# A trunk of three token mixers: gate columns taken beside the RWKV scan, pooling and retention taken as pairs of block products behind it

## The chip, the cores and the metric

One core of one Trainium2 chip runs the whole program. The metric is the device time of one execution in microseconds (us). The kernel before took 2242.8 us as the median of three runs (2242.8 to 2242.94). Engines go by the profile's names: PE is TensorE's matmuls, PEld its weight loads, DVE is VectorE, ACT is ScalarE, POOL is GpSimd, and SP issues all DMAs.

## The reference

Two layers and a final RMSNorm on a sequence of 1024 positions with 1024 channels, float32. A layer is:

```
h = rms_norm(x, norm_g) * (1 + scale) + shift
proj = h @ w_in
o_pool = causal_pool_mixer(pool_u, pool_w, pool_scale) * silu(pool_g)
o_ret  = retention(q, k, v, positions, ret_norm_g) * silu(ret_g)
o_rwkv = rwkv7_time_mix(rw, ...) * silu(rw_g)
y = einsum('btnw,nwd->btnd', stack(o_pool, o_ret, o_rwkv), w_branch)
merged = sum(sigmoid(gate_logits) * y, over branches)
x = x + gate * (merged @ w_out)
```

`proj` has 13 columns of tiles for RWKV (lora, and k, r, v of four pairs of heads), 8 for pooling, 16 for retention (q, k, v and a gate for each of four heads), 4 for the gate of RWKV's output, and 24 for the gate logits. RWKV's state is a recurrence over time. Here it runs in 16 chunks of 64 positions for each pair of heads.

## The kernel before, in words

All large products are float32 kept as a high and a low part (`split`: ACT casts the high part, POOL or DVE subtracts it), so one product of two tiles takes three matmuls of 128x128 by 128x512. A column of w_in is an *item*: `("rq", 2)`, `("gate", 1, 5)` and so on. An item alone (`in_tile2`) is 2 halves of the sequence x 8 tiles x 3 = 48 wide matmuls. Two items together (`forms`) go as a 2x2 block product by 7 instead of 8 block products (`prod`, 12 wide matmuls each), so a pair takes 84 in place of 96. The sums that this needs of the activations (`form`, tiles `T`, `thi`, `tlo`) and of the weights (`wforms`, tiles `wsum`) are made on DVE. The output of a pair ends in PSUM tiles `acc` (three banks in a ring), which `evac` reads out.

A layer goes through these stages. (1) *Scan*: `plan_layer` gives the items lora and k, r, v of the next pair of heads, and, as filler between the steps of the scan, single items. Before, those are pooling's two and retention's four items of each group and head, with the work that follows on them (`pool_task`, `ret_task`). (2) *Pairs*: 14 pairs, before from the 24 gate items and the 4 items of RWKV's output gate. (3) *Branches*: the three branch outputs by w_branch, then the output product.

`rwkv_task` runs one pair of heads: `prepare` (decays, normed keys, from the lora product `lw`), `place` and `scores` (tiles AR, BK, BKt, Z, G), `invert` and `blocks` (the triangular inverse), then the loop of 16 steps. A step is a chain over three engines: PE `two<-S,AR`, DVE `xst`, PE `ch<-xst,G`, ACT `Z`, PE `ch<-Z,BKt`, DVE `S`. The next pair's task begins when this one is done. The big tiles come from four buffers of tag `r8` (AR, BK, BKt, Z, MT: five tiles through four buffers) and one of tag `G`. The smaller ones come from `t_ri` (14), `t_mi` (8) and `t_mo` (4).

The text's order is not the program's order. Each call is recorded as an `Op` with a lane, and `Log.plan` then lists all of them again for five engines, by readiness and a key (place in the text plus a bias of its lane; `rwkv` goes first), with costs of its own. Every recorded instruction is issued in `emit`, so they all carry one line (L550) in the profile. The cost list of `Log.times` has no entry for a load of ACT's function tables, which is put in after the order is set. SP's DMAs are ordered by the same list.

Of the kernel before, what the change touches and what calls it, by code (L numbers as in the profile page):

```python
# [17 lines left out]
P = 128  # L18
D = 1024
T = 1024  # L20
L = 2
# [77 lines left out]
EARLY = (0, 0, 0, 0, 0)  # L99
# [21 lines left out]
RATE = 0.0027  # L121
HOT = ("rwkv", "hot", "lead")
# [3 lines left out]
class Op:  # L126
    __slots__ = (
        "eng", "calls", "port", "outs", "ins_", "lane", "key", "n", "late", "allocs", "after", "took",
        "left", "users", "ready", "start", "end", "occ", "dur", "inst", "no_dep", "own_dep", "idx", "big", "since", "flex", "held", "behind",
# [78 lines left out]
class Log:  # L208


    def __init__(self, nc, tc):
# [7 lines left out]
        self.quiet = None  # L219
        self.real = {"DVE": nc.vector, "POOL": nc.gpsimd}  # L220
# [6 lines left out]
    def call(self, eng, name, real, a, k):  # L227
# [11 lines left out]
        else:  # L239
# [3 lines left out]
            o.no_dep = o.own_dep = o.behind = None  # L243
            o.held = False
# [98 lines left out]
    def plan(self):  # L343
# [32 lines left out]
        for o in todo:  # L376
            o.occ, o.dur = self.times(o)
            o.big = o.eng == "PE" and len(o.calls) == 1 and o.n == "matmul" and o.calls[0][2]["rhs"].dtype == F32R
            o.key = o.idx + BIAS.get(o.lane, 0)
# [184 lines left out]
def trunk_kernel(ctx, tc, xT, cvec, pos, vecs, consts, w_ada, w_all, pool_w, lora_w, out):  # L564
# [407 lines left out]
    keep_w = {}  # L972

# [4 lines left out]
    def plan_layer(l):  # L978
        yield from [("lora",)] + RW(0)
        pools = deque(PL(i) for i in range(4))  # L980
        gates = deque(GT(0, *range(8)) + GT(1, *range(8)) + GT(2, *range(8)))
        done = 0
        while done < 4 or prog.get((l, 3), 0) < 10 or pools:
            if done < 4 and prog.get((l, done), -1) >= 0:
                done += 1
                if done < 4:
                    yield from RW(done)
                if l == 0 and done == 1:
                    yield from pools.popleft()
                yield from RT(done - 1)  # L990
            elif pools and 4 - len(pools) <= done and len(lanes["mix"]) < 2:
                yield from pools.popleft()
            elif 24 - len(gates) < EARLY[done]:
                yield gates.popleft()
            else:
                yield ("idle",)
        yield ("merge",)
        while lanes["rwkv"]:
            yield gates.popleft() if len(gates) > 24 else ("idle",)
        for _ in range(len(gates) % 2):  # L1000
            yield gates.popleft()
        rest = list(gates) + [("wg", i) for i in range(4)]
# [296 lines left out]

    def rwkv_task(l, hp, kT, rT, vp, lt):  # L1300
# [5 lines left out]
        nc.gpsimd.memset(Gf[:, 32 * P : 32 * P + 1], 0.0)  # L1306
        qa = lambda b: slice(64 + 32 * b, 96 + 32 * b)
        BKt = r8("BKt").rearrange("p (c n) -> p c n", n=P)
        Z = r8("Z").rearrange("p (c n) -> p c n", n=P)
# [3 lines left out]
        jt = lambda t, rows, c: t[rows, c, :, :].rearrange("p j t -> p (j t)")  # L1313
        bvs, rks = [], []
        kept_ = [None, None]

        def prepare(h):
            yield wait(*lt[h])
            pss = [mx("lw"), mx("lw")]
            lora_mm(pss, lw, lt[h])  # L1320
# [38 lines left out]
            kept_[h] = Ep, Em, kkn, ka  # L1359

        def place(h):
            cr = slice(8 * h, 8 * h + 8)
            Ep, Em, kkn, ka = kept_[h]
# [5 lines left out]
            for par in range(2):  # L1369
# [14 lines left out]
            nc.vector.scalar_tensor_tensor(  # L1384
                BK[:, cr, 0, :], c3(kkn), -0.5, c3(Em), op0=ALU.mult, op1=ALU.mult
            )
            yield pace()
            nc.vector.tensor_tensor(BK[:, cr, 1, :], c3(ka), c3(Em), op=ALU.mult)
            whole[h] = max(at(AR), at(BK))
            rk = ka  # L1390
            yield pace()
            nc.vector.scalar_tensor_tensor(rk, rT[h], vv(l, "r_k", hp), ka, op0=ALU.mult, op1=ALU.mult)
            yield wait(rk)
            rkh = t_ri("rkh", F32R)
            nc.scalar.copy(rkh, rk)
            rkl = t_ri("rkl", F32R)
            nc.gpsimd.tensor_tensor(rkl, rk, rkh.bitcast(F32), op=ALU.subtract)
            rks.append((rkh, rkl))
# [12 lines left out]
        def scores(h):  # L1411
            yield max(until(whole[h] + 1000), wait(Z, spare=600))
            for q in range(2):
# [3 lines left out]
                with nc.together():  # L1417
                    for c in range(n):
                        trans(ps[:, c * P : (c + 1) * P], jt(BK, slice(0, P), c0 + c), timed=True)
# [3 lines left out]
            with nc.together():  # L1423
                for j in range(8):
                    for hd in range(2):
# [3 lines left out]
                            gps[j // 4 * 2 + hd][:, o : o + P], jt(BK, rows, 8 * h + j), jt(AR, rows, 8 * h + j), timed=True  # L1429
# [9 lines left out]
        yield from prepare(0)  # L1439
        yield from prepare(1)  # L1440
        yield from place(0)
        yield from side(scores(0), place(1))
        nc.gpsimd.memset(Z[0:64, :, :], 0.0)
        yield from scores(1)
        prog[(l, hp)] = 0
        MT = r8("MT")
        M, T1, Lo = two[0:64, :], MT[0:64, 0:1024], MT[0:64, 1024:2048]
        AV = MT[64:128, :]
        T13 = T1[0:32, :].rearrange("p (u s) -> p u s", s=32)
        start = [0.0]  # L1450

        def back(b):
            q = slice(32 * b, 32 * b + 32)
            nc.vector.transpose(
                out=G[q, :, qa(b)].rearrange("p u t -> p t u"), in_=M[q, :].rearrange("p (t s) -> p t s", s=32)
            )

        def invert():
            for b in range(2):
                q = slice(32 * b, 32 * b + 32)  # L1460
                yield pace()
                nc.vector.transpose(
                    out=Lo[q, :].rearrange("p (t s) -> p t s", s=32),
                    in_=G[q, :, qa(b)].rearrange("p u t -> p t u"),
# [71 lines left out]
        for S in SS:  # L1536
            nc.gpsimd.memset(S, 0.0)
# [3 lines left out]
        def outputs(c, cy, behind=None):  # L1541
            if c % 8 == 0:
                ys[c // 8] = t_ri("y")
# [1057 lines left out]
```

## Time and profile before

| | |
|---|---|
| median of the runs | 2242.8 us |
| the profiled execution | 2243.38 us |
| its span, first to last instruction | 2241.6 us |
| PE busy | 2199.1 us, 98% |
| DVE busy | 1661.7 us, 74% |
| ACT busy | 969.0 us, 43% |
| POOL busy | 620.5 us, 28% |
| DMA, mean over the span | 111 GB/s |

The stages of layer 0 lie at about 112 to 652 us (scan), 652 to 929 us (pairs) and 929 to 1120 us (branches, output); those of layer 1 at 1176 to 1740, 1740 to 2012 and 2012 to 2184 us. The granted clock is 1.00, TensorE's upper level of 2.4 GHz, from 112 us to 2184 us. Busy times of PE are modelled, so 98% says that PE has matmuls in hand, and the stretches in which it has none are its idle time.

### The profile page before, as it was taken

How to read it: one execution, taken by the hardware profiler on the slowest of the kernel's cores; microseconds unless marked ns; L12 is line 12 of the kernel's file. 1: busy time of each engine (PE TensorE's matmuls, PEld its weight loads, DVE VectorE, ACT ScalarE, POOL GpSimd, SP SyncE). 2: the span in 40 equal slices, each digit the busy share in tenths (PEclk: the TensorE clock that was granted, in tenths of full speed). 3: DMA queues.
4: the chain of work that ended last, by engine and by line, in shares of the span. 5: the costliest groups of instructions: out<-in, count | busy, mean ns of one | idle time of the engine just before them, and what ended most of it. 6: DMA issues, size and time to landing. Idle time of an engine off the chain costs nothing. (4 is left out here: it accounts for less than half of the span.)

```text
span 2241.6 us, 34653 instructions
## 1 busy us (share of the span) xinstructions
PE 2199.1 (98%) x12788; PEld 1831.4 (82%) x12788; DVE 1661.7 (74%) x2896; ACT 969.0 (43%) x1863; POOL 620.5 (28%) x551
## 2 busy tenths in 40 slices
PE   6999999999999999999999999999999999999998
PEld 5787888888888888888878888888888888888887
DVE  6897888789587764759888788787877644465895
ACT  5636344452344444414464444435334444451254
POOL 2232324233364321420032142233435300041100
PEclk9999999999999999999999999999999999999999
DMA  9212111112146653754450111111213333356343
GB/s 320 70 46 79 39 41 39 50 60 94 50 134 212 211 194 118 239 174 148 139 180 26 49 34 49 43 43 49 85 49 108 123 112 113 113 186 229 116 141 113
DMA packets 139193, 247.77 MB, mean 111 GB/s; under 512 B 15760, under 2 KB 21136, under 8 KB 139024
## 3 DMA queue, kind: packets, MB, share of 16 engines
q1 hardware_dynamic: 139024, 245.56, 34.1%
q8 instruction: 101, 1.65, 0.3%
q14 instruction: 68, 0.56, 0.1%
HBM read 185.99 MB, written 59.51 MB: 110 GB/s over the span
## 5 line engine op out<-in xcount | busy, mean ns | idle before, releaser
L550 PE MATMUL acc<-hhi,wh 128*128 128x512 f32 x1408 | 565.3, 402 | 1.5 <-DVE rot L550 0.8
L550 PE MATMUL acc<-hhi,wl 128*128 128x512 f32 x1408 | 566.2, 402 | 0.0
L550 PE MATMUL acc<-hlo,wh 128*128 128x512 f32 x1408 | 563.5, 400 | 0.0
L550 POOL TENSOR_TENSOR wl<-wr,wh 128x512 fp32r<-128x512 f32 x139 | 185.7, 1336 | 464.6 <-ACT wh L550 332.1
L550 PEld LDWEIGHTS acc<-hhi,wh 128*128 128x128 f32 x1408 | 265.6, 189 | 47.7 <-DVE rot L550 2.0
L550 PEld LDWEIGHTS acc<-hlo,wh 128*128 128x128 f32 x1408 | 265.4, 189 | 45.3
L550 PEld LDWEIGHTS acc<-hhi,wl 128*128 128x128 f32 x1408 | 265.3, 189 | 44.7
L550 ACT CAST wh<-wr 128x512 fp32r<-128x512 f32 x210 | 129.6, 617 | 247.1 <-PE acc L550 175.1
L550 PE MATMUL acc<-T,wh 128*128 128x512 f32 x672 | 208.3, 390 | 0.0
L550 POOL TENSOR_TENSOR wl<-wsum,wh 128x512 fp32r<-128x512 f32 x51 | 74.6, 1464 | 322.1 <-ACT wh L550 322.0
L550 PEld LDWEIGHTS acc<-T,wh 128*128 128x128 f32 x672 | 125.8, 188 | 26.0 <-ACT s L550 0.2
L550 ACT CAST wh<-wsum 128x512 fp32r<-128x512 f32 x128 | 79.4, 621 | 133.3 <-PE acc L550 126.2
L550 PE MATMUL acc<-T,wl 128*128 128x512 f32 x336 | 131.1, 390 | 0.0
L550 DVE TENSOR_TENSOR wl<-wraw,wh 128x512 fp32r<-128x512 f32 x72 | 49.6, 688 | 81.5 <-ACT wh L550 81.5
L550 DVE SCALAR_TENSOR_TENSOR S<-ch,pc,SP 64x64 f32<-64x64 f32 x224 | 63.2, 282 | 56.0 <-PE ch L550 53.0
L550 ACT CAST wh<-wraw 128x512 fp32r<-128x512 f32 x96 | 59.4, 619 | 85.9 <-PE acc L550 38.0
L550 DVE TENSOR_TENSOR wl<-wsum,wh 128x512 fp32r<-128x512 f32 x77 | 53.2, 690 | 58.4 <-ACT wh L550 58.1
L550 ACT ACTIVATE SP<-S,pc 128x128 f32<-128x128 f32 x112 | 44.9, 401 | 99.9 <-DVE S L550 99.0
L550 ACT COPY Z<-ch 64x128 f32<-64x128 f32 x128 | 33.0, 258 | 125.2 <-PE ch L550 124.6
L550 DVE TENSOR_TENSOR two<-two,tm 64x30 f32<-64x30 f32 (+14 forms) x240 | 78.9, 329 | 7.0
L550 DVE TENSOR_TENSOR tm<-MT,two 64x30 f32<-64x30 f32 (+14 forms) x240 | 76.4, 318 | 9.8 <-ACT two L550 2.7
L550 PE MATMUL acc<-oy,wh 128*128 128x512 f32 x256 | 80.2, 394 | 0.0
(343 smaller groups left out, 4977.9 us busy)
## 6 DMA issues: line engine op xcount, KB each, us to landing
wr<-in_w_all SPq DMA_DIRECT2D x230, 256.0 KB, 2.7
wraw<-in_w_all SPq DMA_DIRECT2D x128, 256.0 KB, 2.7
gd<-gsg SPq DMA_DIRECT2D x96, 256.0 KB, 2.0
gs<-gd SPq DMA_DIRECT2D x96, 256.0 KB, 3.4
wada<-in_w_ada SPq DMA_DIRECT2D x80, 256.0 KB, 3.1
ol<-od SPq DMA_DIRECT2D x48, 256.0 KB, 3.4
traw<-hd SPq DMA_DIRECT2D x32, 256.0 KB, 3.0
x<-in_xT SPq DMA_DIRECT2D x16, 256.0 KB, 5.4
```

The costliest lines, as they stand in the source:

```text
L550: o.inst = f(*a, **k)
```

## The change

The plan of items is turned round. Beside the scan now stand the gate items, `QUOTA` = 6 for each pair of heads, all 24 as single items. Pooling and retention, 24 items, and the 4 of RWKV's output gate stand behind the scan as 14 pairs: for each i the pairs (pu, pg), (rq, rv) and (rk, rg), and at the end the four `wg` as two pairs. So both kernels have 24 single items and 14 pairs in a layer.

`rwkv_task` keeps one set of AR, BKt, Z, MT and G for all four pairs of heads of a layer (four `r8` buffers, one `G`). Each pair refills them chunk by chunk, as far as the pair before has read them. BK now lies in four `t_ri` tiles. `prepare` of the next pair is run along with the loop of this one (`overlap`). `rkh` and `rkl` are made in `prepare`, no longer in `place`.

Tiles move between pools: y, yc, ysq and wob from `t_ri` to `t_mi`, gate outputs in the scan from `t_ri` to `t_mi`, and `rot` from `t_mo` to `t_ri`. In a pair whose first item is rq or rk the last sum is written back into PSUM (`acc<-acc,s`), since `rotary` reads its halves there.

```diff
-EARLY = (0, 0, 0, 0, 0)
+QUOTA = (6, 6, 6, 6)
...
     def plan_layer(l):
         yield from [("lora",)] + RW(0)
-        pools = deque(PL(i) for i in range(4))
         gates = deque(GT(0, *range(8)) + GT(1, *range(8)) + GT(2, *range(8)))
...
-                if l == 0 and done == 1:
-                    yield from pools.popleft()
-                yield from RT(done - 1)
-            elif pools and 4 - len(pools) <= done and len(lanes["mix"]) < 2:
-                yield from pools.popleft()
...
+                for _ in range(QUOTA[done - 1]):
+                    yield gates.popleft()
...
-        rest = list(gates) + [("wg", i) for i in range(4)]
+        rest = []
+        for i in range(4):
+            rq, rk, rv, rg = RT(i)
+            rest += PL(i) + [rq, rv, rk, rg]
+        rest += list(gates) + [("wg", i) for i in range(4)]
         yield ("forms", [(rest[i], rest[i + 1]) for i in range(0, len(rest), 2)])
...
     def rwkv_task(l, hp, kT, rT, vp, lt):
-        lw = lora_load(l, hp)
-        AR = r8("AR").rearrange("p (c j t) -> p c j t", j=2, t=CH)
-        BK = r8("BK").rearrange("p (c j t) -> p c j t", j=2, t=CH)
-        Gf = gtile("G")
+        lw = []
+        if hp == 0:
+            scan[l] = r8("AR"), r8("BKt"), r8("Z"), r8("MT"), gtile("G")
+            nc.gpsimd.memset(scan[l][4][:, 32 * P : 32 * P + 1], 0.0)
+        AR, BKt, Z, MT, Gf = scan[l]
...
+            for q in range(2):
+                b = t_ri("BK")
+                BK.append(b)
...
+            def overlap():
+                while not done:
+                    if len(ahead[l]) > hp + 1:
+                        while True:
+                            nc.lower = LOWER
+                            dt = next(ahead[l][hp + 1], None)
+                            nc.lower = 0
+                            if dt is None:
+                                return
+                            yield dt
+                    yield 500
+
+            done = []
+            yield from side(loop(), overlap())
...
             prod(cd, b22, False)
-            nc.vector.tensor_tensor(s2, cd, s2, op=ALU.add)
-            evac(ia, s2, 1)
+            if ia[0] in ("rq", "rk"):
+                nc.vector.tensor_tensor(cd, cd, s2, op=ALU.add)
+                evac(ia, cd, 1)
+            else:
+                nc.vector.tensor_tensor(s2, cd, s2, op=ALU.add)
+                evac(ia, s2, 1)
```

How the orders of the two programs differ is shown at three places. First, ACT in layer 0, from the last copies of the inverse to the second copy of the loop (`G` and `Z` feed PE's next products; `nrot` is the sine of the rotary tables). Before:

```order
L550 COPY G_267<-two 32x16x32
L550 ACTIVATE vp_392<-acc_390,vec_100 128x511
L550 ACTIVATE carry_393<-acc_390,vec_100 128x1
L550 ACT_TABLE_LOAD
L550 ACTIVATE nrot_281<-nrot_281 64x512
L550 COPY G_267<-two 32x16x32
L550 ACTIVATE nrot_281<-ang_280 64x512
L550 COPY Z_269<-ch_417 64x128
```

And in the change:

```order
L553 COPY G_252<-two 32x16x32
L553 ACT_TABLE_LOAD
L553 ACTIVATE nrot_267<-nrot_267 64x512
L553 ACT_TABLE_LOAD
L553 ACTIVATE sg_391<-lw_389,vec_100 128x512
L553 ACTIVATE aT_393<-lw_390,vec_100 128x512
L553 COPY G_252<-two 32x16x32
```

The lora activations of the next pair of heads have come in between the two copies of `G`, with a second table load. Over the program ACT has 10 table loads in place of 8. Both new ones lie here and in the first step of the loop that follows.

Second, PE in layer 0's pairs, at the end of a pair (`rs`, `rkt`, `rvt`, `rkv` and `ro` are retention's products of 128x128). Before, a gate pair:

```order
L550 MATMUL acc_1306<-hhi_224,wl_1320 128x512
L550 MATMUL acc_1307<-thi_1283,wh_1327 128x512
L550 MATMUL acc_1307<-tlo_1284,wh_1327 128x512
L550 MATMUL acc_1307<-thi_1283,wl_1328 128x512
L550 MATMUL acc_1307<-thi_1285,wh_1327 128x512
L550 MATMUL acc_1307<-tlo_1286,wh_1327 128x512
```

In the change, the pair (rk, rg) of head 0:

```order
L553 MATMUL acc_1132<-hhi_224,wl_1148 128x512
L553 MATMUL rs_1176<-rq_1095,rk_1150 128x128 x4
L553 MATMUL rkt_1178<-cst,rk_1150 128x128 x4
L553 MATMUL acc_1133<-thi_1049,wh_1156 128x512
L553 MATMUL acc_1133<-tlo_1050,wh_1156 128x512
L553 MATMUL acc_1133<-thi_1049,wl_1157 128x512
L553 MATMUL acc_1133<-thi_1051,wh_1156 128x512
L553 MATMUL acc_1133<-tlo_1052,wh_1156 128x512
L553 MATMUL rvt_1185<-cst,rv_1126 128x128 x4
```

Retention's and pooling's own products have left the scan and stand between the wide products of the pairs. Over the whole program PE has the same matmuls in both, 10,634 instructions, form by form.

Third, DVE where a PSUM tile with rotary columns is read out. Before, in the loop of layer 0's second pair of heads:

```order
L550 TENSOR_TENSOR rk_682<-acc_670,cs_464 128x512
L550 TENSOR_TENSOR xst<-two,MT_591 64x128
L550 SCALAR_TENSOR_TENSOR ksq_781<-aT_780,ksq_781 128x512
L550 SCALAR_TENSOR_TENSOR rot_683<-acc_670,cs_465 64x512
L550 TENSOR_TENSOR rot_683<-acc_670,cs_465 64x512
```

In the change, in a pair (rq, rv):

```order
L553 SCALAR_TENSOR_TENSOR po_1314<-pps_1313,vec_100,silu_1227 128x512
L553 SCALAR_TENSOR_TENSOR ada_acc_1214<-wada_1216,fixed,ada_acc_1214 128x256
L553 TENSOR_TENSOR acc_1239<-acc_1239,s_1132_1252 128x512
L553 TENSOR_TENSOR wl_1280<-wsum_1278,wh_1279 128x512
L553 TENSOR_TENSOR rq_1276<-acc_1239,cs_1115 128x512
L553 SCALAR_TENSOR_TENSOR rot_1277<-acc_1239,cs_1097 64x512
L553 TENSOR_TENSOR rot_1277<-acc_1239,cs_1097 64x512
```

The three reads of the rotary step no longer stand among `xst` and `S`, the scan's own DVE steps. They stand among the weight sums and the conditioning products (`ada_acc`), with one more sum ahead of them.

## Rows read from the trace of the kernel before

**Rows 1.** Stages: us, PE, PEld, DVE, ACT, POOL busy (count), PE clock, DMA share, GB/s.

```profile
0.00:112.00 112.00, 90.20 (x411) 74.59 (x412) 87.63 (x160) 67.19 (x111) 26.12 (x37) 0.92 0.56 195
112.00:652.00 540.00, 532.52 (x3777) 444.31 (x3777) 439.62 (x879) 235.12 (x500) 184.27 (x175) 1.00 0.20 59
652.00:929.00 277.00, 276.54 (x1265) 229.25 (x1266) 191.72 (x266) 121.26 (x212) 92.51 (x64) 1.00 0.57 183
...
1176.00:1740.00 564.00, 562.05 (x3941) 470.05 (x3941) 448.45 (x868) 242.22 (x515) 193.30 (x183) 1.00 0.17 53
1740.00:2012.00 272.00, 272.00 (x1226) 225.84 (x1225) 138.08 (x193) 121.46 (x214) 53.33 (x38) 1.00 0.39 127
...
sum 2241.60, PE 2199.11 PEld 1831.38 DVE 1661.74 ACT 969.01 POOL 620.53; mean PE 244.35 PEld 203.49 DVE 184.64 ACT 107.67 POOL 68.95
```

**Rows 2.** The same view, a stretch in layer 1's pairs with wide matmuls alone.

```profile
1848.00:1904.00 56.00, 56.00 (x249) 46.37 (x248) 23.35 (x35) 23.56 (x42) 3.87 (x3) 1.00 0.35 112
```

**Rows 3.** What PE waited for, 112 to 652 us: us in total, times, longest.

```profile
PE ch L550 <- DVE xst L550: 1.8, 3, 1.2
PE ch L550 <- ACT Z L550: 1.0, 1, 1.0
...
PE pps L550 <- ACT sg L550: 0.8, 1, 0.8
PE ch L550 <- ACT G L550: 0.7, 1, 0.7
...
PE acc L550 <- DVE rot L550: 0.5, 1, 0.5
```

**Rows 4.** What PE waited for, 1176 to 1740 us.

```profile
PE two L550 <- DVE S L550: 0.8, 2, 0.7
PE ch L550 <- DVE xst L550: 0.6, 2, 0.3
PE acc L550 <- DVE rot L550: 0.3, 1, 0.3
```

**Rows 5.** What PE waited for, 0 to 112 us: the row of the lora product.

```profile
PE lw L550 <- DVE lt L550: 1.3, 1, 1.3
```

**Rows 6.** PE's timeline, 545 to 548 us: start, us, engine, line, operation.

```profile
545.00 0.48 PE L550 MATMUL acc<-hhi,wh 128*128 128x512 f32 x1
545.31 0.39 PE L550 MATMUL acc<-hlo,wh 128*128 128x512 f32 x1
...
547.38 0.39 PE L550 MATMUL acc<-hlo,wh 128*128 128x512 f32 x1
547.61 0.38 PE L550 MATMUL ro<-R,rq 128*128 128x128 f32 x2
547.75 0.47 PE L550 MATMUL acc<-hhi,wl 128*128 128x512 f32 x1
548.06 0.39 PE L550 MATMUL acc<-hhi,wh 128*128 128x512 f32 x1
```

**Rows 7.** Groups of DVE by form: count, busy us, mean ns, idle before.

```profile
L550 DVE SCALAR_TENSOR_TENSOR rot<-acc,cs 64x512 f32<-64x512 f32 x32 | 22.1, 691 | 0.5
...
L550 DVE SCALAR_TENSOR_TENSOR silu<-silu,acc 128x512 f32<-128x512 f32 x32 | 21.5, 676 | 7.3 <-ACT silu L550 7.0
...
L550 DVE SCALAR_TENSOR_TENSOR po<-pps,vec,silu 128x512 f32<-128x512 f32 x16 | 11.9, 747 | 2.8 <-POOL pt L550 2.0 <-PE pps L550 0.4
```

**Rows 8.** Timeline of ACT and PE round a table load, 166 to 169 us.

```profile
166.38 0.24 ACT L550 ACTIVATE carry<-acc,vec 128x1 f32<-128x1 f32 x1
166.64 1.28 ACT L550 ACT_TABLE_LOAD   x1
...
167.93 0.63 ACT L550 ACTIVATE nrot<-nrot 64x512 f32<-64x512 f32 x1
...
169.08 0.33 PE L550 MATMUL ch<-xst,G 128*65 128x64 f32 x2 [0.70 <-ACT G L550]
```

**Rows 9.** DMA issues of the page: count, KB each, us to landing.

```profile
ol<-od SPq DMA_DIRECT2D x48, 256.0 KB, 3.4
```

More of the change, by code (lines that the diff above doesn't have):

```diff
@@ L128 @@
         "eng", "calls", "port", "outs", "ins_", "lane", "key", "n", "late", "allocs", "after", "took",
[L129 removed]
+        "left", "users", "ready", "start", "end", "occ", "dur", "inst", "no_dep", "own_dep", "idx", "big", "since", "flex", "held", "behind", "lower",
     )
@@ L1458, in invert, with main, back @@
-        def invert():
-            for b in range(2):
+        def main():
+            yield from early
+            yield from place(0)
+            yield from side(scores(0), place(1))
+            nc.gpsimd.memset(Z[0:64, :, :], 0.0)
+            yield from scores(1)
+            prog[(l, hp)] = 0
+            M, T1, Lo = two[0:64, :], MT[0:64, 0:1024], MT[0:64, 1024:2048]
+            AV = MT[64:128, :]
+            T13 = T1[0:32, :].rearrange("p (u s) -> p u s", s=32)
+            start = [0.0]
+            def back(b):
@@ new lines, in states @@
+            def states():
+                for q in range(4):
+                    yield wait(G, Z)
+                    ps = mx("av")
+                    with nc.together():
+                        for j in range(8):
+                            c, hd = 4 * q + j // 2, j % 2
+                            u0 = (16 * hd + c) * P + 64
+                            n = 65
+                            mmul(ps[0:n, j * 64 : j * 64 + 64], Gf[:, u0 : u0 + n], Z[:, c, 64 * hd : 64 * hd + 64])
+                    nc.scalar.copy(AV[:, q * HF : (q + 1) * HF], ps[0:64, :])
+                    yield 1500
@@ new lines, in main, with outputs @@
+            ys = [None, None]
+            def outputs(c, cy, behind=None):
+                if c % 8 == 0:
+                    ys[c // 8] = mi("y")
+                y = ys[c // 8]
+                with nc.together():
+                    for hd in range(2):
+                        cols = slice(64 * hd, 64 * hd + 64)
+                        o = mmul(
+                            cy[0:65, cols],
+                            G[:, 16 * hd + c, 0:65],
+                            Z[:, c, cols],
+                            start=c == 0,
+                            skip_group_check=True,
+                        )
+                if behind is not None:
+                    o.after[behind] = 2
+                o = (c % 8) // 2 * P
+                r = slice(64 * (c % 2), 64 * (c % 2) + 64)
+                nc.scalar.copy(y[r, o : o + P], cy[0:64, 0:P])
+                if c % 8 == 7:
+                    h = c // 8
+                    yn = layer_norm(y, 8, 64, RWKV_EPS, mi, nc.gpsimd)
+                    posts[l, hp, h] = add("post", rwkv_post(l, hp, h, yn, bvs[h]))
@@ L1604, in rwkv_post, with both @@
+        def both():
+            yield from prepare(0)
+            yield from prepare(1)
+        early = both()
+        ahead[l].append(early)
+        return main()
     def rwkv_post(l, hp, h, yn, bv):
```

329 lines of the change are left out of this document (147 added, 182 removed).

## The prediction

> **What bounds the kernel now.** I read the stages first, then what PE waited for, then the timeline at single waits. PE is busy 2199.1 of 2241.6 us [rows 1], so it lacks matmuls for 42.5 us in all. 21.8 us of that lie in the lead-in before 112 us. The scan of layer 0 has 540.0 - 532.5 = 7.5 us, its pairs 0.5 us, the scan of layer 1 has 1.95 us and its pairs nothing [rows 1]. The rest, 42.5 - 31.7 = 10.8 us, lies at the change of layer and at the end, where the order of PE's rows is the same in both kernels. In a stretch of wide matmuls alone 249 go in 56 us, which is 0.225 us each with no gap [rows 2]. PE is therefore the bound in every stage, and an engine that gets faster beside it gives nothing but PE's idle time. What this change can win at most is the idle time of the stages that it rearranges: 7.5 + 0.5 + 1.95, about 10 us, and a part of the lead-in.
>
> **The change, part by part.** The profiled execution took 2243.4 us (span 2241.6 and 1.8 around it), 0.6 us over the median. The sum is made against 2243.4.
>
> *PE's work.* A layer has 24 single items at 48 wide matmuls and 14 pairs at 84, before and after. Which columns are paired changes, not how many. The order of both programs has the same 10,634 matmuls. This term is 0. Per layer, retention's 212 products of 128x128 and pooling's 24 wide ones move from the scan to the pairs. A 128x128 product in float32 stands as two records 0.11 us apart, 0.22 us, so 212 x 0.22 + 24 x 0.225 = 52 us of PE's time move with them: the scan gets shorter by that, the pairs longer.
>
> *Entries into narrow work.* In PE's order a narrow run breaks into wide matmuls 602 times, before 561 times: 41 more. From 547.38 to 548.06 a wide one, a narrow product and a wide one take 0.68 us, where 2 x 0.225 + 0.22 = 0.67 would be due; the other end is a wide matmul behind a narrow run that took 0.31 in place of 0.225 [rows 6]. So the price is 0.01 to 0.085 us, 0.4 to 3.5 us for 41. I take 0.4, since the runs that move are retention's, as in the first row.
>
> *Lead-in.* The first lora product waited 1.3 us for its operand [rows 5]. In the change three more wide matmuls stand ahead of it, 0.7 us. So -0.7, between -1.3 and 0.
>
> *Scan of layer 0.* Out go the waits that belong to pooling and rotary columns: 0.8 of `pps` and 0.5 of `rot` [rows 3]. VectorE's load falls. What moves from it are two groups of about 22 us for `rot`, 21.5 us for `silu`, and twelve groups of pooling, retention and their norms of 11 to 16 us, of which `po` with 11.9 is a usual one [rows 7]: 44 + 21.5 + 12 x 11.9 = 208 us, 104 a layer. Its share of the scan was 439.6/540 = 81% [rows 1] and becomes (439.6 - 104)/(540 - 52) = 69%. I take a third off the 1.8 us for `xst`, 0.6. Together -1.9.
>
> In come two table loads. The loop of the first pair of heads had four, now it has six. At 166.64 us a load of 1.28 us ahead of the copy of `G` cost PE 0.70 us; a copy of `Z` had a wait of 1.0 us [rows 8, 3]. At two places the change has two loads in front of one such copy. PE's order gives the chain no more cover than before: 4 wide matmuls (0.9 us) between `two` and `ch`, 4 between `ch` and the product with BKt, 6 between that and the next `two`, in both programs. The first load of a place has eaten that cover, so I charge the second one in full: +2 x 1.28 = +2.6. Its ends are 0 (hidden) and 2.6. The stage comes to +0.7, between -7.5 (all waits gone) and +2.6.
>
> By the Trainium skill ("ScalarE: Activation LUTs", What ACT_TABLE_LOAD costs) a switch of tables costs a drain of some 1.38 us beside the load of 1.28, 2.66 us in all, and that speaks against this change. In the trace the load begins 0.02 us after the end of the instruction before it and the next begins 0.01 us behind it [rows 8], so no drain shows. By the page the two new loads would be 5.3 us, and the sum 2.7 us higher.
>
> *Scan of layer 1.* It has no table loads. The waits are 0.8 for `S`, 0.6 for `xst` and 0.3 for `rot` [rows 4]. The last goes, and half of the others with VectorE's load: -1.0, between -1.95 and 0.
>
> *Pairs.* Here the 104 us of VectorE arrive. Its share in layer 0 was 191.7/277 = 69% and becomes 296/329 = 90%; in layer 1 51% becomes 242/324 = 75% [rows 1]. (Some of its weight splits go over to POOL, which has room, so this is the upper side.) The nearest rows are the pairs of layer 0 at 69%, with 0.5 us idle in 277, and the scan of layer 0 at 81%, with 7.5 in 540. On 653 us of pairs that is 1.1 us by the first rate; by the second for layer 0 and layer 1's scan rate (1.95/564) for layer 1 it is 4.6 + 1.1 = 5.7 us. I take 2, near the lower end, as the cover is longer. A rotary column is read out of its PSUM bank by one sum and three reads of about 0.69 us each [rows 7], 2.8 us, and the bank is wanted again 24 wide matmuls later, 5.4 us; in the scan the cover was 0.9 us.
>
> *Costed at nothing.* The last half of retention ends late: its store stands in SP's queue ahead of the loads for the second half of the first branch. Between its transposes (`rot`) and the first product on those loads stand 51 wide matmuls, 11.5 us; a load lands in 3.4 us [rows 9]. If that cover went, each late load would be PE's idle time one to one. The refill of AR, BKt and Z by chunks adds waits on reads of the pair before, but each of the 15 passes from step to step keeps at least 10 wide matmuls, so they wait beside PE's work. The stores of the gates move forward; SP issues 963 DMAs in both, and where the stores now lie DMA is busy 20% [rows 1].
>
> Sum: 0 + 0.4 - 0.7 + 0.7 - 1.0 + 2.0 = +1.4 us, 2244.8 beside 2243.4, and by the median **2244.2 us**. The ends of all terms together are 2242.8 + (0.4 - 1.3 - 7.5 - 1.95 + 0) = 2232.5 and 2242.8 + (3.5 + 0 + 2.6 + 0 + 5.7) = 2254.6.
>
> **The rivals.** *The waits of the scan vanish.* VectorE at 69% let PE wait 0.5 us in 277 in the pairs [rows 1]. If the scan behaves like that, its waits fall to about 1 us in each layer, and only the table loads' 1.7 us [rows 3] stay. Then 7.5 + 1.95 becomes 3.7, with 1.1 in the pairs, 0.4 for entries and -0.7 in the lead-in: -5.7 + 0.8 = -4.9 us, **2237.9**. For it speaks that in the second half of each loop VectorE has little but `xst` and `S` left in the new order; against it that the chain's cover on PE has not grown.
>
> *The rotary columns hold PSUM (the other sign).* The cover of 5.4 us less the 2.8 us of the read-out leaves 2.6 us for the queue ahead on VectorE. In the new order weight splits, weight sums and, in layer 0, conditioning products stand among these reads. If the queue is later than 2.6 us, each of the 16 rotary pairs stops PE. At 0.6 us each, what a `rot` wait came to in the scan (0.5 and 0.3 [rows 3, 4], with the added sum), that is +10 us in place of the +2: **2252**. The point is VectorE's share: it decides above some 90% in layer 0's pairs. For it speaks the 90% worked out above, against it the splits that went to POOL.
>
> *A table load costs twice its row.* With a drain behind each of the two new loads the sum is 2244.2 + 2.7 = **2246.9**; that is the page's rule above. The rows show no drain.
>
> *The change does not do what it says.* If `prepare` of the next pair did not fit into the loop, the chain of heads would not get shorter. As filler does not run out in either order, that would leave the time at **2243**, within the forecast.
>
> **How the numbers follow.** A measurement of this kernel can tell 0.2% from no change, 4.5 us: 2238.3 to 2247.3. Forecast with the last rival in it 0.50, vanishing waits 0.22, rotary columns 0.19, costly table loads 0.09. Vanishing waits lie half beyond the lower bound by the spread of their terms, and I give 0.17 of the 0.22 to it as the lower ends reach far; with 0.04 from the forecast's own lower end, faster is 0.21. Rotary columns give 0.19, costly loads 0.04 and the forecast's upper end 0.04: slower is 0.27. The same is 0.52. The range takes in the first rival down to 2235, as not all of its waits need stay, and the second up to 2252: **2235 to 2252**. Beyond it lie the last of both, some 2 in 10.
>
> **What would show it.** PE's idle time in the first loop of layer 0 with waits of about 2 us on `G` and `Z` right behind the table loads; the scan of layer 0 ending some 50 us earlier, at about 600 us; VectorE at 85 to 90% in layer 0's pairs and PE's idle time there of 1 to 3 us. The forecast is wrong if PE's busy time itself moves by more than 4 us, if the pairs show a wait on `rot` or `acc` at every pair, or if PE's idle time falls below 37 us in all.

## The result, and the profile after

The change takes 2247.05 us (median of 19 runs, 2244.94 to 2251.39); the kernel before, run beside it, 2242.49 us (19 runs). The ratio is 1.0022, with a 95% interval of 1.0015 to 1.0029: some 5 us slower, a small loss, but clear of no change. The forecast was 2244.2 us in a range of 2235 to 2252. The profiled execution of the change took 2245.94 us, with a span of 2244.2 us.

The stages of the change, in the same columns as [rows 1]:

```profile
0.00:112.00 112.00, 93.92 (x414) 77.87 (x416) 90.73 (x167) 68.04 (x113) 25.38 (x36) 0.98 0.59 200
112.00:608.00 496.00, 489.82 (x3456) 406.76 (x3453) 357.54 (x728) 228.21 (x488) 115.58 (x109) 1.00 0.25 79
608.00:927.00 319.00, 316.49 (x1579) 264.64 (x1578) 281.23 (x403) 123.48 (x218) 184.93 (x139) 1.00 0.42 127
...
1176.00:1704.00 528.00, 525.58 (x3645) 437.43 (x3644) 363.88 (x729) 235.08 (x504) 134.97 (x126) 1.00 0.24 74
1704.00:2010.00 306.00, 304.42 (x1501) 254.34 (x1500) 219.80 (x312) 124.23 (x218) 158.46 (x121) 1.00 0.26 78
```

The first product on T comes at 608 us instead of 655, and VectorE's share there is 357.5/496 = 72% (81% before); in the pairs it is 281.2/319 = 88% (69%). PE has no matmul for 6.2, 2.5, 2.4 and 1.6 us in the four stages behind the lead-in, where [rows 1] had 7.5, 0.5, 1.95 and 0 (1.5 of the third belong to the turn of the layers, at 1182 us). What PE waited for in the change, in four stretches one after the other: 112 to 608, 608 to 927, 1120 to 1205 and 1704 to 2010 us.

```profile
PE ch L553 <- ACT Z L553: 2.6, 2, 2.1
PE nps L553 <- ACT sg L553: 1.8, 1, 1.8
PE ch L553 <- DVE xst L553: 1.1, 2, 0.6
...
PE acc L553 <- ACT s L553: 1.2, 1, 1.2
PE ro L553 <- DVE R L553: 0.7, 2, 0.4
PE rkt L553 <- DVE po L553: 0.4, 1, 0.4
...
PE acc L553 <- POOL hlo L553: 1.5, 1, 1.5
...
PE rot L553 <- DVE yc L553: 0.8, 1, 0.8
PE acc L553 <- DVE s L553: 0.6, 1, 0.6
```

The waits on `pps` and `rot` of [rows 3] are gone, two longer ones on ACT (`Z` 2.1 and `sg` 1.8 us) have come, and the pairs and the turn of the layers have waits that [rows 1] left no room for. The timeline shows three of these places: ACT and PE at the table loads of layer 0; PE at the start of its pairs; POOL at the turn of layers.

```profile
165.93 1.28 ACT L553 ACT_TABLE_LOAD   x1
167.22 0.63 ACT L553 ACTIVATE nrot<-nrot 64x512 f32<-64x512 f32 x1
167.87 1.28 ACT L553 ACT_TABLE_LOAD   x1
169.16 0.69 ACT L553 ACTIVATE sg<-lw,vec 128x512 f32<-128x512 f32 x1
...
169.90 0.50 PE L553 MATMUL nps<-ksh,bone 128*128 128x512 f32 x1 [1.78 <-ACT sg L553]
...
616.15 0.39 PE L553 MATMUL acc<-hhi,wl 128*128 128x512 f32 x1
617.70 0.50 PE L553 MATMUL acc<-T,wh 128*128 128x512 f32 x1 [1.16 <-ACT s L553]
...
1177.53 3.03 POOL L553 TENSOR_TENSOR wl<-wr,wh 128x512 fp32r<-128x512 f32 x1 [7.62 <-DVE ka L553]
1180.53 1.72 POOL L553 TENSOR_TENSOR rkl<-ka,rkh 128x512 fp32r<-128x512 f32 x1
1182.21 1.78 POOL L553 TENSOR_TENSOR hlo<-xres,hhi 128x512 fp32r<-128x512 f32 x1
```

The idle time that a profile shows does not hold all that a wait costs. From 616.15 to 617.70 are 1.55 us: the matmul itself is worth 0.225 [rows 2], the wait is shown as 1.16, and 0.165 are left, which is what its record runs on beyond the moment when the next one could have begun (0.39 - 0.225). So I compare stages by their **excess**: the stage's time less that of its matmuls at the undisturbed rate (0.2265 us a wide one, 0.110 a record of 128x128, and in the same way for the smaller forms). It holds idle time, the short delays that no idle time shows, and what a lower clock costs. The undisturbed sum over the program is 2129.6 us before and 2129.7 after, so PE's work is indeed the same. Excess in us, by stage, each time of the one profiled execution of a run. The lead-in begins with PE's first matmul and the scan with the first transpose of a layer's BK; the pairs begin with the first product on T and end with the first on `oz`; the turn lies between the layers, and the tail ends with PE's last matmul. The branches, where the excess is 1.2 to 3.1 us in all of these runs, are left out.

| | lead-in | scan 0 | pairs 0 | turn | scan 1 | pairs 1 | tail |
|---|---|---|---|---|---|---|---|
| before (its second execution) | 30.4 | 31.2 | 2.0 | 4.6 | 22.2 | 0.4 | 2.6 |
| the change | 31.0 | 26.2 | 7.4 | 6.1 | 19.3 | 5.1 | 2.2 |
| sines together | 30.9 | 27.1 | 13.0 | 6.4 | 19.6 | 4.6 | 2.1 |
| sums in pairs (on before) | 30.4 | 32.2 | 7.8 | 4.6 | 22.2 | 0.5 | 2.2 |
| sums in scan (on the change) | 29.9 | 33.3 | 10.7 | 5.4 | 21.0 | 11.9 | 2.4 |
| later narrow | 30.4 | 26.2 | 9.2 | 6.1 | 19.5 | 2.4 | 4.9 |
| one more pair | 31.2 | 26.1 | 7.3 | 6.1 | 19.2 | 7.6 | 3.1 |
| three edits | 29.3 | 26.2 | 10.4 | 4.9 | 18.9 | 2.3 | 3.3 |
| two edits | 30.6 | 26.1 | 7.5 | 5.0 | 18.9 | 2.3 | 7.9 |

So the scans gained 5.0 and 2.9 us, the pairs lost 5.4 and 4.7, the turn 1.4; the rest (lead-in, branches) some 1 us. The loss is what is left over between two larger movements. Where the order of PE is the same, single executions agree well: before's first execution has 1.9 and 0.4 us in its pairs, and the last row has layer 0 in the order of the change. The lead-in and the tail vary more.

### The profile page after: what moved, and what is told of

Its sections match the earlier page's. It is cut to its first block, busy times and chain, and to the rows that moved or that the text cites. A ratio compares the mean times of both kernels' runs of the same rounds, so it can differ in the third digit from the quotient of the medians.

```text
span 2244.2 us, 34723 instructions
## 1 busy us (share of the span) xinstructions
PE 2202.3 (98%) x12788; PEld 1833.6 (82%) x12788; DVE 1677.7 (75%) x2880; ACT 969.3 (43%) x1865; POOL 702.5 (31%) x593
## 4 chain that ended last, share of the span: by engine, by line
PE 88%; DVE 7%; ACT 2%; issue 1%; DMA 1%; POOL 0%; SPq 0%; DVEq 0%; POOLq 0%; ACTq 0%
PE acc L553 71%; PE two L553 3%; PE ch L553 3%; PE av L553 1%; PE ro L553 1%; DVE ksq L553 1%; DVE two L553 1%; DVE tm L553 1%; PE m L553 1%; PE g L553 1%; PE rs L553 1%; PE bt L553 1%; PE rkv L553 0%; PE pps L553 0%; DMA x<-in_xT 0%
## 5 line engine op out<-in xcount | busy, mean ns | idle before, releaser
L553 POOL TENSOR_TENSOR wl<-wr,wh 128x512 fp32r<-128x512 f32 x127 | 169.9, 1337 | 574.8 <-ACT wh L553 379.8
L553 PE MATMUL acc<-T,wh 128*128 128x512 f32 x672 | 214.5, 394 | 1.2 <-ACT s L553 1.2
L553 POOL TENSOR_TENSOR wl<-wsum,wh 128x512 fp32r<-128x512 f32 x80 | 109.7, 1371 | 141.7 <-ACT wh L553 105.1
L553 POOL TENSOR_TENSOR wl<-wraw,wh 128x512 fp32r<-128x512 f32 x57 | 84.8, 1487 | 56.9 <-ACT wh L553 52.5
L553 DVE TENSOR_TENSOR xst<-two,MT 64x128 f32<-64x128 f32 x120 | 35.1, 293 | 79.7 <-PE two L553 78.5
L553 ACT ACTIVATE gsg<-acc 128x512 f32<-128x512 f32 x96 | 57.0, 595 | 82.4 <-PE acc L553 81.5
```

Source lines behind the costliest of these rows:

```text
L553: o.inst = f(*a, **k)
```

## The experiments

**The kernel before, again.** It served as the measure of a difference of nothing.

> The kernel before, unchanged, for a second profile and a spread. All theories: ratio 1.000 within 0.001. The change's profile had 4 us less idle time of PE in the lead-in (11.3 against 15.2 us) with the same rows there. If that is the change's doing, this profile has 15 us again, and what happens behind the lead-in costs 4.6 + 4 = 8 us. If it is chance (when the first loads land), it will be anywhere from 11 to 15 us.

2242.21 us, ratio 0.9999 (0.999 to 1.0008). The shorter idle time in the lead-in of the change need not come from the change: up to 104 us PE has no matmul for 21.8 and 21.3 us in two executions of before, for 18.3 and 18.5 in the two other runs with before's lead-in (sums and first form in the pairs, below), and for 18.1 in the change.

**The two sines under one table load.** The two `nrot` activations go as one group, so that ACT has 8 table loads in place of 10.

```diff
-            nc.scalar.activation(n[0:64, :], n[0:64, :], AF.Sin)
-            nc.scalar.activation(n[64:128, :], ang[64:128, :], AF.Sin)
+            with nc.together():
+                nc.scalar.activation(n[0:64, :], n[0:64, :], AF.Sin)
+                nc.scalar.activation(n[64:128, :], ang[64:128, :], AF.Sin)
```

> The change, with the two sines of each half of the rotary tables issued one behind the other, so that ACT has 8 table loads as before, not 10. Theory 1 (the two added loads stand on the path of the first loop of layer 0, waits of 1.8 us on the norm product and 2.1 us on Z): 2.5 to 4 us faster than the change, 2243 to 2244.5 us, and one of the two long waits gone. Theory 2 (the loss is in the pairs): within 1 us of the change, 2246 to 2248 us.

2248.54 us, ratio 1.0028 (1.0017 to 1.0039): no gain; the 2.5 us or more of the first theory did not come. PE's idle time in scan 0 fell from 6.2 to 4.6 us, yet its one wait at the loads, 2.4 us, was followed by this (PE's clock is the third number from the right):

```profile
160.00:168.00 8.00, 7.84 (x129) 6.20 (x126) 7.81 (x13) 4.65 (x7) 0.36 (x1) 1.00 0.21 68
168.00:176.00 8.00, 5.73 (x16) 4.64 (x17) 2.52 (x5) 5.97 (x11) 0.00 (x0) 0.57 0.31 84
176.00:184.00 8.00, 8.00 (x53) 6.78 (x53) 7.78 (x14) 6.52 (x15) 0.00 (x0) 1.00 0.12 42
```

Inside that wait, which lasted from 167.84 to 170.27 us, the granted clock fell to 0.50, TensorE's lower level of 1.2 GHz, and stayed there from 168.9 to 175.7 us; 0.57 is the mean of the 8 us. The planner also gave PE another order from 177 us on: only 9 wide matmuls stood between the last scan product of layer 0 and the first product on T (28 in the change), and pairs 0 lost 5.6 us more. So this run does not tell what the two loads cost by themselves.

**Each half of the change alone.** First the scan of the change with the items in the old places (`plan_layer` of before, with EARLY), then the scan of before with the gates as filler and the new pairs.

> The new scan (one set of tiles for all pairs of heads, prepare of the next pair beside the loop) with the old plan: pooling and retention beside the scan, gates in pairs. Theory 1 (overlap and its table loads cost): it has 8 loads, so at most half of the loss, 2244 us or less; theory 2 (narrow products between the wide ones of the pairs and their read-outs cost): no loss at all, 2240 to 2243 us, as nothing narrow stands in the pairs. PE's order has 530 entries into narrow runs against 561 before and 602 in the change; at 0.086 us, the mean of the scan's excess for each, that is 2.7 us less than before: 2240 us. Theory 3 (the two parts only pay together, since prepare and retention crowd VectorE in the loop): slower than the change, over 2248 us.

> The old scan with the new plan: gates beside the scan, pooling and retention in pairs. Theory 2 (the pairs lose): the loss stays, 2246 to 2249 us, with 2 to 3 us idle in the pairs of layer 0 and 1 to 2 in those of layer 1. Theory 1 (overlap and table loads lose): 2242 to 2244 us. It has 10 table loads too, but at other places.

2302.77 us (ratio 1.027, 1.0256 to 1.0284) and 2267.9 us (1.011, 1.0096 to 1.0124). The first is slower, as its third theory had it; the second lies above both of its theories. In the first order the products on T begin before the last product of the scan in both layers, in the second in layer 0: the filler runs out, and the chain of the scan lies bare. The waits of the first, in all:

```profile
PE two L554 <- DVE S L554: 10.0, 11, 2.0
...
PE ch L554 <- DVE xst L554: 5.6, 11, 1.3
PE acc L554 <- DVE T L554: 4.5, 2, 2.3
PE rkt L554 <- DVE rsm L554: 3.7, 1, 3.7
```

and its clock at the end of scan 0:

```profile
640.00:652.00 12.00, 9.86 (x79) 8.40 (x77) 7.44 (x18) 4.97 (x14) 2.16 (x2) 1.00 0.22 66
652.00:656.00 4.00, 1.74 (x13) 1.34 (x12) 2.97 (x8) 1.00 (x4) 2.05 (x2) 0.79 0.22 66
656.00:684.00 28.00, 20.75 (x97) 16.27 (x96) 11.90 (x28) 9.45 (x26) 4.90 (x6) 0.50 0.16 50
684.00:692.00 8.00, 5.70 (x25) 4.13 (x23) 5.30 (x11) 6.11 (x13) 5.82 (x5) 0.94 0.19 59
```

Neither half can stand alone in this planner, and what the change costs cannot be put down to one of them. That a shorter scan needs filler with less work of its own is how I read it; no run shows that by itself.

**VectorE's share in the pairs.** Before's pairs get VectorE sums but no narrow products. A first form read the gate's own sum three times more, which for half of the gate halves still lay in its `acc` bank and for the others in the SBUF tile `s`.

```diff
             nc.scalar.activation(s, ps, AF.Tanh, scale=0.5)
+            for _ in range(3):
+                nc.vector.scalar_tensor_tensor(s, ps, 0.0, s, op0=ALU.mult, op1=ALU.add)
```

> The kernel before, with three VectorE sums of 128x512 added to each half of a gate column (48 halves a layer, 3 x 0.69 us each, about 99 us a layer), all of them in the pairs, where before has its gates. They add 0 x the PSUM tile to the gate tile, so the values stay. No narrow product is moved. In the two traces so far the pairs' time over that of their matmuls at full rate (called excess here) rose from 1.9 to 7.4 us in layer 0 and from 0.4 to 5.1 us in layer 1. Theory A (the moved narrow products meet operands that have just been made): this kernel's pairs stay near 2 and 1 us and the time is 2242 to 2245 us. Theory B (VectorE's higher share in the pairs costs PE its time): the pairs go to 7 and 5 us, the time to 2250 us or more.

2316.41 us, ratio 1.0327 (1.0311 to 1.0343): far over both. The dose was too large for layer 0, (191.7 + 98)/277 = 105% of VectorE; but layer 1, at 87%, lost still more (44.6 us of excess, against 33.7). Layer 1's waits in the pairs:

```profile
PE acc L550 <- DVE gsg L550: 12.5, 10, 1.3
PE acc L550 <- ACT acc L550: 12.2, 12, 1.0
```

They are waits for a bank that `gsg`'s sums read, or for ACT's copy into one. In layer 1 the granted clock fell as well: its mean is 0.99 in layer 0's pairs (306 us) and 0.96 in layer 1's (314 us), an estimated 3 and 13 us. Without that the two layers lose about the same, 31 and 32 us, at 105% and 87%. So this run shows the price of PSUM banks that are read for 2 us more, not that of VectorE's share. The second form reads a tile that the pairs don't use, in a smaller dose.

```diff
+            for _ in range(2 if l else 2 - h):
+                nc.vector.scalar_tensor_tensor(s, two[:, 0:HF], 0.0, s, op0=ALU.mult, op1=ALU.add)
```

> The kernel before, with VectorE sums of 128x512 added to the gate halves in the pairs, as in the run with three such sums but fewer of them, and reading a PSUM tile that the pairs do not use, so that no acc bank is held: three for each gate column in layer 0 (72 x 0.68 = 49 us), four in layer 1 (96 x 0.68 = 65 us). They add 0 x that tile to the gate tile, so the values stay. VectorE's share of the pairs becomes (191.7 + 49)/277 = 87% and (138.1 + 65)/272 = 75%; the change has 88% and 72%. Theory A (the loss in the pairs is waits and entries of the narrow products): the excess of the pairs stays at 2 to 3 us and 0.5 to 1 us, the time at 2243 to 2245 us. Theory B (VectorE's share alone): 7 and 5 us, 2251 us.

2247.55 us, ratio 1.0024 (1.0014 to 1.0035). Its pairs, layer 0 and layer 1:

```profile
652.00:932.00 280.00, 275.71 (x1252) 226.18 (x1251) 231.05 (x313) 119.00 (x210) 116.50 (x85) 1.00 0.56 178
...
1740.00:2015.00 275.00, 275.00 (x1239) 228.22 (x1238) 186.47 (x266) 122.21 (x215) 85.16 (x63) 1.00 0.38 125
```

The time lies between the two theories, and each is right in one layer. In layer 0 more work on VectorE, to 231/280 = 83%, is enough by itself to cost 5.8 us: the excess goes from 2.0 to 7.8 us without one more narrow product (the planner put some of PE's products elsewhere from 665 us on), in short waits on many tiles (`s`, `ada_acc`, `T`, `wh`, none over 0.8 us). That this is what costs the change 5.4 us there is not shown: at 88% it has 2.5 us without a matmul in these pairs, this run 4.3. In layer 1, at 186/275 = 68% (72% in the change), nothing is lost, and PE has not a moment without a matmul.

**VectorE's share in the scan.** The change gets 33 and 66 us of VectorE's work back beside the scans.

```diff
+            for _ in range(1 + l):
+                nc.vector.tensor_tensor(s, s, s, op=ALU.max)
```

A larger dose, that of the first form above, was run too:

> The change, with the same three VectorE sums at each half of a gate column, all of them in the scan, where the change has its gates: about 99 us a layer, what retention and pooling took away from VectorE there. The excess of the scans fell with the change from 31.2 to 26.2 us (layer 0) and from 22.3 to 19.3 us (layer 1). Theory D (the scan gained because VectorE's load fell): the excess goes back to about 31 and 22 us and the time to 2255 us. Theory E (it gained because the next pair's prepare no longer stands between two loops): the excess stays at 26 and 19 us, the time at 2247 to 2249 us.

2323.04 us, ratio 1.0364 (1.035 to 1.0379), with 21.3 us of PE waits on the bank (`acc<-gsg`): it says no more than its sister did. The smaller one:

> The change, with VectorE maxima of 128x512 of the gate tile with itself (the values stay) at each gate half of the scan, one in layer 0 (48 x 0.69 = 33 us) and two in layer 1 (96 x 0.69 = 66 us); they read SBUF alone and hold no acc bank. VectorE's share of the scans goes from 72% to (357.5 + 33)/496 = 79% and from 69% to (363.9 + 66)/528 = 81%, which is where before had it (81% and 80%). Theory D (the scan gained because VectorE's load fell): the excess goes back to about 31 and 22 us, the time to 2255 us. Theory E (it gained because prepare runs beside the loop): 26 and 19 us, 2247 to 2249 us.

2263.3 us, ratio 1.0099 (1.0085 to 1.0112), above both theories. Scan 0 has 33.3 us of excess. The granted clock from 168 to 176 and from 180 to 188 us was 0.84, 0.73, 0.62 and 0.95 in pieces of 4 us, which is 4 x (0.16 + 0.27 + 0.38 + 0.05) = 3.4 us lost, by estimate, behind the waits at the table loads. Without it 29.9 are left, 3.7 of the 5.0 us that the change had won. In layer 1 it is 1.6 of 2.9 us. So VectorE work of about the former size takes back most of the scans' gain in layer 0 and about half in layer 1. This does not prove that the gain came from there. The planner gave PE another order from 159 us on, and what comes back is of another kind: in layer 0 2.8 us of idle time, where the change had won 1.3. What `prepare` beside the loop gives was not tried by itself. Some 10 us more of this run's loss lie in the pairs. There the first product on T stands ahead of the last scan product in layer 0, and only 24 wide matmuls behind it in layer 1 (28 and 97 in the change), which leaves the sums for T less time.

**Narrow products later.** 1.2 us more margin in the planner for the products of retention, pooling and the scan's end.

```diff
-                    gap += MARGIN
+                    gap += MARGIN + (1200 if u.lane in ("mix", "post") else 0)
```

> The change, with 1.2 us more margin in the planner between the end of an operand on another engine and the PE product of retention, pooling and the scan's end that reads it. The order has the same matmuls, 593 entries into narrow runs in place of 602. Theory A (short waits on operands just made): the excess of the pairs falls from 7.4 and 5.1 us to some 4 and 2 us, the time to about 2242 us. Theory C (each entry has a price of its own, about 0.07 us): 9 entries fewer, -0.6 us, 2246.4 us. Theory B (VectorE's share): no change, 2247 us.

2246.44 us, ratio 1.0017 (1.0008 to 1.0026). Pairs 1 go from 5.1 to 2.4 us, with no idle time left; pairs 0 from 7.4 to 9.2. Theory A holds for layer 1 and not for layer 0. That the time is the 2246.4 us of theory C is chance: it is made up of movements in both directions. 45 runs of narrow products are left in pairs 1 without any idle time of PE, and cost 2.4 us: some 0.05 us each at most, and not the 0.07 of theory C.

**One more pair.** `QUOTA = ((6, 6, 6, 6), (6, 6, 6, 4))` takes 12 wide matmuls out of layer 1.

> The change, with 4 in place of 6 gate columns beside the last pair of heads of layer 1: 22 single items and 15 pairs there, so 12 wide matmuls fewer, 12 x 0.225 = 2.7 us. In the order the first product of the pairs stands 4 wide matmuls ahead of the last scan product (97 behind it in the change). Theory F (the filler was longer than the scan of layer 1 needed): -2.7 us, 2244.3 us. Rival (the scan's end runs out of cover): waits of 2 us or more on the scan's chain at the end of layer 1's scan, 2246 us or above.

2247.21 us, ratio 1.0021 (1.0012 to 1.0029): the undisturbed sum fell by 2.7 us to 2127.0, and pairs 1 gave 2.5 of it back (7.6 for 5.1). The scan had no new waits; the first pair had (`acc<-T`, `yt<-yc`), as its first product on T now stands 3 wide matmuls ahead of the last scan product, no longer 97 behind it. As I read these waits, the spare matmuls were the time in which the sums for T were made.

**Three edits, and two of them.** Retention's products into `ro` in one group; the margin in layer 1 alone; the first `rkl` of layer 1 on VectorE, since on POOL it stood ahead of `hlo` (1180.53 to 1182.21 us above, itself behind a weight split of 3.03 us). The second run leaves out the group of `ro`.

```diff
-                    gap += MARGIN
+                    gap += MARGIN + u.more
...
-            for c in range(4):
...
+            with nc.together():
+                for c in range(4):
...
-            nc.gpsimd.tensor_tensor(rkl, rk, rkh.bitcast(F32), op=ALU.subtract)
+            (nc.vector if l and not hp else nc.gpsimd).tensor_tensor(rkl, rk, rkh.bitcast(F32), op=ALU.subtract)
...
+        nc.more = 1200 * l
```

> The change with one edit for each wait that the trace of it shows. Retention's products into ro go as one group (21 and 10 entries into ro become at most 8 and 8; 2.1 us of excess in layer 0 stood at them); the margin of 1.2 us for retention's and pooling's products in layer 1 alone (its pairs went from 5.1 to 2.4 us with it); the first rkl of layer 1 on VectorE in place of GpSimd, where it stood ahead of the last hlo (a wait of 1.5 us). Theory A: -1.7, -2.7 and -1.4 us, together 2241 us, which is 1.5 us below before. Rival (each edit only moves the waits to other products, as the margin did in layer 0's pairs, +1.8 us): 2244 us or above.

> As the run with three edits, with ro's products single again: the margin of 1.2 us in layer 1 and the first rkl of layer 1 on VectorE are left. The order of layer 0 is that of the change, row by row. Two theories of layer 0's pairs, whose excess was 7.4 us in the change and 10.4 us with ro grouped: with theory B for layer 0 (VectorE at 88% is late wherever an order needs it, and a new order only moves the waits) it returns to 7.4 us, the excess of layer 1's pairs stays at 2.4 us and that of the turn of layers at 4.9 us. The time is then 2240.6 us, counted from the run with three edits (2243.6 - 3.0), or 2243.2 us, counted from the change (2247.05 - 2.7 - 1.1); the first would be below before. Rival (the waits of layer 0's pairs come from the turn of layers or from run to run, not from the order): 10 us there again and 2243.6 us.

2243.59 us (ratio 1.0011, 1.0002 to 1.002) and 2244.22 us (1.0006, 0.9997 to 1.0015). The times do not tell these two apart; the stages do. The margin did what it should (2.3 us in pairs 1) and the new place of `rkl` nearly so (the turn 4.9 for 6.1 us). The group of `ro` did the opposite: pairs 0 went to 10.4 us, with a new wait of 1.8 us on `pdh`, and without the group they are back at 7.5. None of the three new orders of layer 0 that were tried (sines together, later narrow, `ro` grouped) lowered the excess of its pairs. By its stages up to the tail the last kernel should have come out at 2241 to 2243 us; its profiled execution, with 2246.69 us the second longest of 11, has 7.9 us of excess in the tail, where the other rows have 2.1 to 4.9. There PE waited 2.1 us for VectorE's `ssum`, and then:

```profile
2212.00:2218.90 6.90, 4.81 (x41) 4.63 (x40) 3.96 (x8) 1.62 (x5) 1.29 (x1) 1.00 0.50 189
2218.90:2226.00 7.10, 7.10 (x35) 7.10 (x36) 2.44 (x8) 1.52 (x6) 0.72 (x1) 0.53 0.00 0
2226.00:2234.00 8.00, 8.00 (x69) 8.00 (x68) 3.44 (x9) 2.78 (x6) 0.00 (x0) 0.99 0.40 134
```

VectorE was late there since it waited 2.6 us for a store of `fin` to give its buffer back. The times on record speak for something that comes and goes within this kernel: its five executions with a mean granted clock of 0.996 or 0.997 took 2241.4 to 2244.2 us (median 2242.2), the six with 0.993 to 0.995 took 2243.4 to 2247.9 (median 2245.2). Where the clock fell in the others is not on record, since only one was profiled. The two edits take back so much of the change's loss that no clear difference from before is left, but no version that is clearly below before was found.

## Why the prediction was right, and where it was not

**PE's work, 0:** right, 2129.6 and 2129.7 us.

**The moved work, 52 and 104 us:** both too large. Of the 212 products, 92 are transposes (`rkt`, `rvt`, `rot`), and a transpose stands as one record of 0.11 us in the trace, not two. So 120 x 0.22 + 92 x 0.11 + 24 x 0.225 = 42 us move. The first product on T came 47 us earlier, of which 5 are excess. VectorE lost 82 and 85 us of work in the scans and not 104. The shares still came out near, 72% and 88% for 69% and 90%.

**Entries into narrow work, +0.4:** the net came out, the reason is not shown. What of the excess is not idle time fell by 3.7 and 2.2 us in the scans and rose by 3.4 and 3.1 in the pairs, +0.6 in all. That looks as if it moved with the narrow products. But some of it is the 0.165 us that a wait costs beside its idle time, and VectorE's load moves it too: with the sums in the pairs of layer 0 it rose by 2.0 us, with those in the scan of layer 1 by 1.7.

**Lead-in, -0.7:** not seen. The wait of `lw` [rows 5] is gone, but the excess of the lead-in is 30.4 and 32.6 in two executions of before and 31.0 in the change; a difference of this size is lost in that.

**Table loads, +2.6:** the size is right, the way only in part. The two places had waits of 0.70 [rows 8] and 1.0 [rows 3] and have 1.78 and 2.12 us: +2.2. The prediction's sign named `G` and `Z`; PE waited for `sg`, by a product of `prepare`, and for `Z`. At the second place the load is over at 177.43 us, and the copy of `Z` begins at 179.60, behind four activations, three of them of `prepare`:

```profile
176.15 1.28 ACT L553 ACT_TABLE_LOAD   x1
177.44 0.63 ACT L553 ACTIVATE Lc<-Lc 128x512 f32<-128x512 f32 x1
177.98 0.58 ACT L553 ACTIVATE gsg<-acc 128x512 f32<-128x512 f32 x1
178.46 0.68 ACT L553 ACTIVATE sg<-lw,vec 128x512 f32<-128x512 f32 x1
179.03 0.69 ACT L553 ACTIVATE aT<-lw,vec 128x512 f32<-128x512 f32 x1
179.60 0.25 ACT L553 COPY Z<-ch 64x128 f32<-64x128 f32 x1
...
179.90 0.49 PE L553 MATMUL ch<-Z,BKt 128*128 128x128 f32 x2 [2.12 <-ACT Z L553]
```

So this wait is not the load alone. The loads at 165.93 and 167.87 us follow their neighbours within 0.03 us again. So the drain that the Trainium skill ("ScalarE: Activation LUTs", What ACT_TABLE_LOAD costs) adds to a load does not show here, and the third rival did not come.

**Scan of layer 0, waits, -1.9:** too small. The 0.8 of `pps`, which I took off with pooling, stood behind a table load too. In before:

```profile
171.69 1.28 ACT L550 ACT_TABLE_LOAD   x1
172.98 0.69 ACT L550 ACTIVATE sg<-lw,vec 128x512 f32<-128x512 f32 x1
...
173.72 0.50 PE L550 MATMUL pps<-pdh,pw 128*128 128x512 f32 x1 [0.81 <-ACT sg L550]
```

Leaving out all waits behind loads, 0.70, 0.81 and 1.0 before and 1.78, 2.12 and 0.49 after, PE's idle time in scan 0 fell from 5.0 to 1.8 us, where I had taken off 1.1. The first rival was right about this half: `xst` waits 1.1 where it had 1.8, and `rot` and most small ones went.

**Scan of layer 1, -1.0:** right as idle time, 1.95 to 0.9 us; the excess fell by 2.9.

**Pairs, +2.0:** the step that failed, by its size. Idle time rose by 2.05 and 1.6 us, 3.6 in all, and the excess by 10.1; I had priced idle time alone. I took a value near the lower end "as the cover is longer". For layer 0's 329 us my two rates give 0.6 and 4.6 us of idle time. The change has 2.5, and the sums in the pairs, at 83% of VectorE, have 4.3. In layer 1 two waits on operands just made, 0.8 and 0.6 us, are nearly all the idle time. A later place takes them away and with them 2.7 of the 4.7 us of excess. What the 5.4 us of layer 0 are made of stays open: VectorE's load can cost that much, but no run takes it away.

**The rotary columns (second rival):** did not come. No wait of PE for a read by `rot`, `rq` or `rk` shows in the pairs of either layer, though VectorE has 88%. That banks held for 2 us longer do stop PE is what the first form of the sums showed; one more sum and three reads behind 24 matmuls of cover were not enough.

**Costed at nothing, and not nothing:** `rkl`. I had not followed POOL's queue at the turn of layers: there `rkl` stands ahead of `hlo`, for which PE waits 1.5 us. The turn lost 1.4 us, half of the 3 us by which the forecast was short, and 1.2 of them went when VectorE took the first `rkl`. The late store of retention cost little, if anything: the branches lost under 1 us.

So the sum came out within its range in part by luck: its wrong terms have opposite signs. In idle time the scans have -2.3 in place of -0.3 and the pairs +3.6 in place of +2.0. In excess the movements are larger still, -7.9 in the scans and +10.1 in the pairs, and the turn adds 1.4 where the sum had nothing. The forecast had the direction of each, and not the size. That `prepare` would not fit into the loop, the last rival, is not told apart by the time, which lay within the forecast; the scan of before with the new items, 2267.9 us, speaks against it. None of the three signs that the prediction named against itself came: PE's busy time moved by 3.2 us, no wait stands at every pair, and PE's idle time is 41.9 us.

## What to carry to other kernels

Price a stage that receives moved work by its time over that of its matmuls, and not by PE's idle time alone: here the idle time of the pairs rose by 3.6 us and their excess by 10.1. A longer cover was no reason for the lower of two prices. Follow every instruction of a moved step to its new neighbours on each queue, GpSimd's too, where a subtraction of 128x512 took 1.7 to 3.0 us at the turn of layers. Where each half of a change is far worse alone (here +60 and +25 us, together +5), a small edit to the order can as well move the waits as remove them: of five here, the margin in layer 1 and the place of `rkl` removed some, and the sines, the margin in layer 0 and the group of `ro` did not.

## What the runs showed of the hardware

A wait of PE can cost far more than itself. In "sines together" the granted clock fell inside a wait of 2.4 us and was 0.50, TensorE's lower level of 1.2 GHz, from 168.9 to 175.7 us; there a wide matmul followed the one before it by 0.43 us and not 0.23. In "two edits" it was 0.50 from 2219.4 to 2226.1 us, right behind a wait of 2.1 us that ended at 2218.90. By estimate, half of the time that PE worked at this level is lost: some 3 us for each. In the sums in the scan it fell behind waits of 1.79 and 1.76 us. After one of 2.12 us at 180 us in the change it stayed at 1.00:

```profile
172.00:180.00 8.00, 5.88 (x34) 4.35 (x32) 6.33 (x9) 7.65 (x14) 0.00 (x0) 1.00 0.26 75
180.00:188.00 8.00, 8.00 (x47) 6.71 (x48) 7.32 (x14) 5.74 (x13) 1.29 (x1) 1.00 0.01 5
```

And with the scan's chain laid bare (the scan of the change kept alone) it stood at 0.50 from 656 to 684 us, with PE busy for 20.75 of these 28 us. So in these runs a wait of about 2 us is a risk rather than a price. The change has two such waits in layer 0's scan, where before had none over 1.2 us; whether some of its executions pay for them is not shown, since only one was profiled.
